# A first stage in another order: squares summed per part, one product to spread a row, both halves of a modulation product in one block

## The chip, the cores and the metric

The kernel runs on one core of a Trainium2 chip. Its engines each take their own instructions in the order in which the program gives them and wait for one another by semaphores: TensorE (PE; its weight loads are shown as PEld), VectorE (DVE), ScalarE (ACT), GpSimd (POOL) and SyncE (SP), which here only issues DMA transfers. The metric is the device time of one execution in microseconds.

## The reference, cut to what matters

One block of a hybrid network over 256 latent tokens, with 256 context tokens ahead of one branch. The change lies in the first lines: the modulation by c, the RMS norm, and the first 1024 columns of the input projection, which alone are needed for both streams.

```python
mod = silu(c) @ w_ada + b_ada                       # (1, 6144): shift, scale, gate
shift, scale, gate = split(mod, 3)                  # mod_c the same from c_ctx
h  = _rmsnorm(x,   norm_g) * (1.0 + scale)   + shift    # x:   256 x 2048
hc = _rmsnorm(ctx, norm_g) * (1.0 + scale_c) + shift_c  # ctx: 256 x 2048
cols = _split_cols(h @ w_in)                        # 13312 columns
xa_c = hc @ w_in[:, :1024]
# RG-LRU over (xa_c, cols[0]), pooling mixer, conformer convolution, each gated by SiLU,
# three projections merged by sigmoid gates, output projection, then
x = x + gate * out
return _rmsnorm(x, final_g)
```

`_rmsnorm(x, g)` is `x * rsqrt(mean(x*x) + 1e-6) * g`. All is float32; a wide product is taken as three products of rounded parts (high x high, high x low, low x high).

## The kernel before, in words

Channels lie on the 128 partitions, in 16 blocks kt of 128 channels; the 512 tokens (256 latent, 256 context) lie along the free axis. xT holds the transposed input as 16 x 512 floats a partition and comes in four transfers, `x_parts`, of 5, 5, 4 and 2 blocks (L376 to L378). cin, 16 KB, holds c and c_ctx; a tanh on ACT (L388) and two operations on DVE make the SiLU of it in sc.

The first stage is one straight list of instructions (`manual_schedule`), so the order of the code is the order on each engine:

1. Squares of each part on ACT (L446), summed over the part's blocks on DVE by a tree of additions, and added to `fold` (L441 to L454).
2. `ada_mm("A", 0)`: half of the product of sc with the modulation weights of block 0, eight matmuls in four column groups. Four small products of `fold` with ones give each token's sum (`tok`, L459); DVE and ACT make the reciprocal root `rt` of it (L461, L462). `ada_mm("B", 0)` is the other half. `keep_warm` issues products that nobody reads.
3. Four times, the diagonal of `rt` and a product with ones (L468, L469) spread one 128-token piece of the row over all partitions; ACT copies it to `rows`.
4. `modulation(kt)` sums the four column groups (L414, L415) and makes shift and gain of a block; `modulate(kt)` multiplies xT by `rows`, applies gain and shift, and splits the result into hH (rounded, ACT) and hL (the rest, DVE).
5. For each kt, seven output tiles of 128 channels: `mm3` issues the three products of a tile, 128x512 each, one behind the other into the same PSUM bank (L239 to L241). Between tiles stand `ada_mm("A", kt + 2)`, `ada_mm("B", kt + 2)` and the modulation of kt + 1.

`Feed` loads weights in a fixed list from SP: each item has a slot, and a load is issued when the slot's holder has been released. `feed.split` makes the rounded and the rest part of a loaded item (ACT, then DVE).

After this stage a list of steps works on the rest of the projections, with the other branches' work in the background of DVE and ACT. The order of these instructions is the same in both kernels.

Of the kernel before, what the change touches and what calls it, by code (L numbers as in the profile page):

```python
# [13 lines left out]
ALU = mybir.AluOpType  # L14

P = 128
D = 2048
KT = 16
L = 256
EPS = 1e-6  # L20
WINDOWS = (2, 4, 8, 16)
NXA = 7
# [12 lines left out]
A_SQ0, A_XT, A_H, A_S, A_RAW = 0, 8192, 16384, 17408, 17920  # L35
# [110 lines left out]
def hybrid_block_kernel(  # L146
# [22 lines left out]
    nc = tc.nc  # L169
# [64 lines left out]
    def split(H, Lo, src):  # L234
        A.copy(H, src)  # L235
        tt(Lo, src, H.bitcast(F32), ALU.subtract)
# [134 lines left out]
    with tc.manual_schedule():  # L371

        cin = sml[:, 0:32]
        nc.sync.dma_start(cin, cc)
        xT = ar[:, A_XT:A_XT + 8192].rearrange("p (k s) -> p k s", k=KT)
        x_parts = ((0, 5), (5, 10), (10, 14), (14, 16))  # L376
        for a, b in x_parts:
            nc.sync.dma_start(xT[:, a:b, :], xt[:, a:b, :])  # L378
        nc.sync.dma_start(vt, vec)
        feed.load()  # L380

# [14 lines left out]
        def mod_ps(kt):  # L396
            return mod_bank[:, 256 * (kt % 2):256 * (kt % 2 + 1)]

        def ada_mm(part, kt):
            i = p1_items[part, kt]  # L400
            ps = mod_ps(kt)
            raw = feed.items[i]["raw"].rearrange("p (k c) -> p k c", c=256)
            for q in range(8):
                k = q if part == "A" else 8 + q
                j = k % 4
                T.matmul(ps[32 * j:32 * j + 32, :], sc[:, k, :], raw[:, q, :], start=k < 4, stop=k >= 12)  # L406
            feed.release(i)
            if part == "B":
                A.copy(S_t[kt % 2], ps)

        def modulation(kt):
            ps = mod_ps(kt)
# [6 lines left out]
            ts(gg, ps[:, 2:4], vt[:, V_BSC + kt:V_BSC + kt + 1], 1.0, op0=ALU.add, op1=ALU.add)  # L419
            ts(gg, gg, vt[:, V_G + kt:V_G + kt + 1], None)  # L420

        def modulate(kt):
            b0 = 80 + 8 * (kt % 2)
            sh, gg = sml[:, b0:b0 + 2], sml[:, b0 + 2:b0 + 4]
            h = h_t[kt % 2]
            tt(h, xT[:, kt, :], rows, ALU.mult)
            for s in range(2):
                hs = h[:, 256 * s:256 * (s + 1)]
                ts(hs, hs, gg[:, s:s + 1], sh[:, s:s + 1])
            split(hH[:, kt, :], hL[:, kt, :], h)  # L430

        warm = bank()

        def keep_warm(n):

            for _ in range(n):
                T.matmul(warm, ones, xT[:, 10, :], start=True, stop=True)
# [3 lines left out]
        tok = bank()  # L441
        for n, (a, b) in enumerate(x_parts):
            k = b - a
            o = A_SQ0 + 2560 * (n % 2)
            sq = ar[:, o:o + 512 * k]
            A.activation(sq, xT[:, a:b, :].rearrange("p k s -> p (k s)"), AF.Square)  # L446
            while k > 1:
                m = k // 2
                tt(sq[:, 0:512 * m], sq[:, 0:512 * m], sq[:, 512 * (k - m):512 * k], ALU.add)
                k -= m  # L450
            if n == 0:
                V.tensor_copy(fold, sq[:, 0:512])
            else:
                tt(fold, fold, sq[:, 0:512], ALU.add)  # L454
        feed.limit = len(feed.items)
        keep_warm(3)
        ada_mm("A", 0)
        for t in range(4):
            T.matmul(tok[:, 2 * t:2 * t + 2], fold[:, P * t:P * (t + 1)], ones[:, 0:2], start=True, stop=True)  # L459
        var, rt, tmp = sml[:, 64:68], sml[:, 68:72], sml[:, 72:76]  # L460
        ts(var, tok[:, 0:8].rearrange("p (t s) -> p t s", s=2)[:, :, 0], 1.0 / D, EPS)  # L461
        rsqrt_newton(rt, var, tmp, rt)  # L462
        ada_mm("B", 0)
        keep_warm(3)
        row_ps = bank()
        for t in range(4):
            w = slice(P * t, P * (t + 1))
            ts(fold[:, w], ident, rt[:, t:t + 1], None)  # L468
            T.matmul(row_ps[:, w], ones, fold[:, w], start=True, stop=True)  # L469
        feed.split(p1_items["X", 0], sub, 1)  # L470
        A.copy(rows, row_ps)
        modulation(0)
        modulate(0)
        feed.split(p1_items["X", 0], sub)
        ada_mm("A", 1)


        xa_ps = [bank() for _ in range(6)] + [small_bank() for _ in range(NXA - 6)]
        for kt in range(KT):
            wh, wl = feed.items[p1_items["X", kt // 2]]["parts"][kt % 2]  # L480
            for t in range(NXA):
                w = slice(P * t, P * (t + 1))
                mm3(xa_ps[t], wh[:, w], wl[:, w], hH[:, kt, :], hL[:, kt, :], kt == 0, kt == KT - 1)
                if t == 1 and kt == 0:
                    ada_mm("B", 1)
                if t == (3 if kt == 0 else 0) and kt + 1 < KT:
                    modulation(kt + 1)
                    modulate(kt + 1)
                    if kt % 2 == 1:
                        feed.split(p1_items["X", (kt + 1) // 2], sub)  # L490
                if t == 0 and kt == KT - 1:
                    feed.split(steps[0][2], sub)
                if t == (4 if kt == 0 else 3) and kt + 2 < KT:
                    ada_mm("A", kt + 2)
            if kt + 2 < KT:
                ada_mm("B", kt + 2)


        xap = [ar[:, A_XAP + 518 * t:A_XAP + 518 * (t + 1)].rearrange("p (s l) -> p s l", s=2) for t in range(8)]
# [712 lines left out]
```

## Time and profile before

| | us |
|---|---|
| median of 3 runs (973.13 to 975.0) | 974.91 |
| the profiled execution's own time | 974.82 |
| its span | 973.0 |
| PE busy in the span | 946.5 (97%) |
| DVE busy | 743.3 (76%) |
| ACT busy | 492.8 (51%) |
| first wide product of the first stage starts at | 28.67 |
| first product of the steps behind it starts at | 149.43 |

The span is what the instructions of the profile cover; some 1.8 us of the execution lie around it. Times in the profile are counted from the start of the span. A line such as L210 or L84 is often that of a helper, so the names of the tiles tell more than the line.

### The profile page before, as it was taken

The page shows a single profiled execution, that of the slowest core. Times are in us where ns is not written, and L with a number is a line of the kernel's source. Part 1 is how long each engine was busy: PE and PEld are TensorE (multiplying, and loading weights), DVE is VectorE, ACT ScalarE, POOL GpSimd, SP SyncE. Part 2 cuts the span into 40 slices and gives each one's busy share as a digit, 9 for nine tenths or more (in the row PEclk, how much of TensorE's full clock was granted, in tenths as well). Part 3 has the DMA queues.
Part 4 walks back from the last instruction along what each step waited for, and adds up shares of the span by engine and source line. Part 5 has one row for each costly group of instructions (what it writes and reads, how often), then busy time and mean ns, then how long its engine had stood idle before and what let it go on. Part 6 is the DMA issues. An engine that isn't in the chain of part 4 may idle for free.

```text
span 973.0 us, 18156 instructions
## 1 busy us (share of the span) xinstructions
PE 946.5 (97%) x7561; PEld 876.6 (90%) x7561; DVE 743.3 (76%) x1143; ACT 492.8 (51%) x641; POOL 40.7 (4%) x74
## 2 busy tenths in 40 slices
PE   4999999999999999999999999999999999999996
PEld 2666668999999999999999999999999999998885
DVE  5445456876976785899999999996666888898764
ACT  4222226566656767674445544444675444444442
POOL 0000010000100000000000000000002011101000
PEclk9999999999999999999999999999999999999998
DMA  9998854554545555455555555555569788878642
GB/s 369 372 416 319 347 191 167 213 173 162 192 168 185 182 187 177 169 186 176 215 180 210 177 213 178 208 180 190 173 204 357 262 320 318 307 262 308 201 173 87
DMA packets 34722, 220.70 MB, mean 227 GB/s; under 512 B 4128, under 2 KB 4272, under 8 KB 11856
## 3 DMA queue, kind: packets, MB, share of 16 engines
q1 hardware_dynamic: 28080, 195.28, 55.1%
q0 software_dynamic: 6560, 24.26, 7.2%
q8 instruction: 59, 0.97, 0.4%
q14 instruction: 23, 0.19, 0.1%
HBM read 217.43 MB, written 2.10 MB: 226 GB/s over the span
## 4 chain that ended last, share of the span: by engine, by line
PE 95%; DVE 2%; DMA 1%; ACT 1%; issue 0%; SPq 0%; ACTq 0%; DVEq 0%
PE acc L265 24%; PE acc L266 24%; PE acc L269 24%; PE sm L406 3%; PE acc L239 3%; PE acc L1100 3%; PE acc L1098 3%; PE acc L1101 3%; PE acc L240 2%; PE acc L241 2%; PE sm L240 1%; DVE ar L210 1%; PE sm L239 1%; PE sm L241 1%; DMA ar<-in_xt_dram 1%; PE acc L960 0%
## 5 line engine op out<-in xcount | busy, mean ns | idle before, releaser
L265 PE MATMUL acc<-hH,wh 128*128 128x256 f32 (+1 forms) x2000 | 466.8, 278 | 0.0
L266 PE MATMUL acc<-hL,wh 128*128 128x256 f32 (+1 forms) x2000 | 464.6, 277 | 0.0
L84 ACT CAST wh<-raws 128x1024 fp32r<-128x1024 f32 (+1 forms) x288 | 298.2, 1050 | 261.5 <-PE acc L266 222.6
L210 DVE TENSOR_TENSOR wl<-raws,wh 128x1024 fp32r<-128x1024 f32 (+1 forms) x288 | 339.7, 1218 | 108.6 <-ACT wh L84 55.5
L265 PEld LDWEIGHTS acc<-hH,wh 128*128 128x128 f32 x2000 | 375.6, 188 | 1.7
L266 PEld LDWEIGHTS acc<-hL,wh 128*128 128x128 f32 x2000 | 375.7, 188 | 0.7
L269 PE MATMUL acc<-hH,wl 128*128 128x256 f32 (+1 forms) x2000 | 253.4, 277 | 0.0
L269 PEld LDWEIGHTS acc<-hH,wl 128*128 128x128 f32 x2000 | 239.5, 188 | 0.7
L221 DVE SCALAR_TENSOR_TENSOR ar<-ar,vt 128x256 f32<-128x256 f32 (+1 forms) x264 | 115.3, 503 | 0.0
L210 DVE TENSOR_TENSOR ar<-ar 128x512 f32<-128x512 f32 (+6 forms) x136 | 87.4, 665 | 7.9 <-ACT ar L446 6.2
L221 DVE SCALAR_TENSOR_TENSOR ar<-ar,sc 128x512 f32<-128x512 f32 x64 | 48.1, 751 | 16.4 <-DMA ar<-in_w_gate_dram 15.0
L235 ACT CAST hH<-ar 128x256 fp32r<-128x256 f32 (+1 forms) x68 | 31.5, 491 | 53.3 <-DVE ar L217 47.0
L210 DVE TENSOR_TENSOR hL<-ar,hH 128x256 fp32r<-128x256 f32 (+1 forms) x76 | 39.5, 547 | 22.7 <-ACT hH L235 22.7
L1100 PE MATMUL acc<-wh,hH 128*128 128x512 f32 (+1 forms) x144 | 51.8, 369 | 0.0
L1101 PE MATMUL acc<-wh,hL 128*128 128x512 f32 (+1 forms) x144 | 51.3, 366 | 0.0
L239 PE MATMUL acc<-hH,wh 128*128 128x512 f32 x96 | 42.5, 442 | 1.2 <-ACT hH L235 1.2
L215 DVE TENSOR_SCALAR sml<-sm,vt 128x2 f32<-128x2 f32 x16 | 3.5, 220 | 48.5 <-PE sm L415 48.5
L240 PE MATMUL acc<-hL,wh 128*128 128x512 f32 x96 | 38.2, 398 | 0.3 <-DVE hL L210 0.2
L241 PE MATMUL acc<-hH,wl 128*128 128x512 f32 x96 | 37.9, 395 | 0.0
L239 PEld LDWEIGHTS acc<-hH,wh 128*128 128x128 f32 x96 | 18.0, 188 | 16.0 <-issue 11.9
L1098 PE MATMUL acc<-wl,hH 128*128 128x512 f32 (+1 forms) x144 | 32.1, 366 | 0.0
L1101 PEld LDWEIGHTS acc<-wh,hL 128*128 128x128 f32 x144 | 27.0, 188 | 4.8 <-issue 0.2
(142 smaller groups left out, 662.4 us busy)
## 6 DMA issues: line engine op xcount, KB each, us to landing
raws<-in_w_br_dram SPq DMA_DIRECT2D x49, 1024.0 KB, 4.9
raws<-in_w_gl_dram SPq DMA_DIRECT2D x48, 1024.0 KB, 4.9
raws<-in_w_bout_dram SPq DMA_DIRECT2D x24, 1024.0 KB, 4.9
raws<-in_w_ada_dram SPq DMA_DIRECT2D x16, 1024.0 KB, 8.9
ar<-in_w_ada_dram SPq DMA_DIRECT2D x16, 1024.0 KB, 8.8
ar<-in_w_gate_dram POOLq DMA_DIRECT2D x32, 512.0 KB, 5.7
raws<-in_w_out_dram SPq DMA_DIRECT2D x16, 1024.0 KB, 5.0
ar<-in_w_xa_dram SPq DMA_DIRECT2D x5, 896.0 KB, 11.7
```

The source lines that it names most:

```text
L84: self.nc.scalar.copy(h[:, 0:w], src)
L210: V.tensor_tensor(out=o, in0=a, in1=b, op=op)
L221: V.scalar_tensor_tensor(o, a, s, b, op0=op0, op1=op1)
L239: T.matmul(ps, sh, mh, start=start, stop=False)
L240: T.matmul(ps, sh, ml, start=False, stop=False)
L241: T.matmul(ps, sl, mh, start=False, stop=stop)
L265: T.matmul(ps, wh[k], mh[k], start=k == 0, stop=False)
L266: T.matmul(ps, wh[k], ml[k], start=False, stop=False)
L269: T.matmul(ps, wl[k], mh[k], start=False, stop=k == len(wh) - 1)
L1098: T.matmul(ps, H, wl[:, w], start=False, stop=kt == KT - 1)
L1100: T.matmul(ps, H, wh[:, w], start=kt == 0, stop=False)
L1101: T.matmul(ps, Lo, wh[:, w], start=False, stop=False)
```

## The change

The transfer of cin is issued behind the four parts of xT and not ahead of them. The sums of squares are no longer added up in `fold`: each part's sum goes through its own four token products, and a reduction on DVE adds the four results. Each part has its own room for the squares. One multiplication on DVE makes the four diagonals, and one 128x512 product spreads the row. Both halves of `ada_mm` stand in one block; the multiplication of xT by the row is issued one block ahead (`scaled`), for block 0 straight from PSUM. The first weights are split behind block 0's modulation. The wide products of a block run over the seven tiles for each of the three pairs of operands.

```diff
-        nc.sync.dma_start(cin, cc)
         x_parts = ((0, 5), (5, 10), (10, 14), (14, 16))
         for a, b in x_parts:
             nc.sync.dma_start(xT[:, a:b, :], xt[:, a:b, :])
+        nc.sync.dma_start(cin, cc)
...
+        def ada_mm(kt):
             ps = mod_ps(kt)
+            for part in "AB":
...
+            A.copy(S_t[kt % 2], ps)
...
+        def scaled(kt, by):
+            tt(h_t[kt % 2], xT[:, kt, :], by, ALU.mult)
...
             split(hH[:, kt, :], hL[:, kt, :], h)
+            if kt + 1 < KT:
+                scaled(kt + 1, rows)
...
-            o = A_SQ0 + 2560 * (n % 2)
+            o = (A_SQ0, A_SQ0 + 2560, A_SQ0 + 5120, A_H)[n]
...
+            for t in range(4):
+                c = 8 * n + 2 * t
+                T.matmul(tok[:, c:c + 2], sq[:, P * t:P * (t + 1)], ones[:, 0:2], start=True, stop=True)
             if n == 0:
-                V.tensor_copy(fold, sq[:, 0:512])
-            else:
-                tt(fold, fold, sq[:, 0:512], ALU.add)
+                keep_warm(2)
...
-        keep_warm(3)
-        ada_mm("A", 0)
...
+        V.tensor_reduce(var, tok[:, 0:32].rearrange("p (n t s) -> p t n s", n=4, t=4)[:, :, :, 0],
+                        axis=mybir.AxisListType.X, op=ALU.add)
+        ts(var, var, 1.0 / D, EPS)
         rsqrt_newton(rt, var, tmp, rt)
-        ada_mm("B", 0)
-        keep_warm(3)
+        tt(fold.rearrange("p (t c) -> p t c", t=4), ident[:, None, :].to_broadcast([P, 4, P]),
+           rt[:, :, None].to_broadcast([P, 4, P]), ALU.mult)
+        keep_warm(2)
         row_ps = bank()
-        for t in range(4):
-            w = slice(P * t, P * (t + 1))
-            ts(fold[:, w], ident, rt[:, t:t + 1], None)
-            T.matmul(row_ps[:, w], ones, fold[:, w], start=True, stop=True)
-        feed.split(p1_items["X", 0], sub, 1)
+        T.matmul(row_ps, ones, fold, start=True, stop=True)
+        ada_mm(0)
+        scaled(0, row_ps)
+        modulation(0)
         A.copy(rows, row_ps)
-        modulation(0)
         modulate(0)
         feed.split(p1_items["X", 0], sub)
-        ada_mm("A", 1)
...
+            at_ada, at_mod = ((5, 20), 10) if kt == 0 else ((13,), 2)
+            for i in range(3 * NXA):
+                a, t = divmod(i, NXA)
+                T.matmul(xa_ps[t], (wh, wh, wl)[a][:, P * t:P * (t + 1)], (hH, hL, hH)[a][:, kt, :],
+                         start=kt == 0 and a == 0, stop=kt == KT - 1 and a == 2)
```

On SP, at the start of the program; cc is cin's tensor, xt the input, vec the small vectors.

```order
-L374 DMA sml<-in_cc_dram 128x32
-L378 DMA ar<-in_xt_dram 128x2560 x2
-L378 DMA ar<-in_xt_dram 128x2048
-L378 DMA ar<-in_xt_dram 128x1024
+L1210 UNCONDITIONAL_BRANCH
+L377 DMA ar<-in_xt_dram 128x2560 x2
+L377 DMA ar<-in_xt_dram 128x2048
+L377 DMA ar<-in_xt_dram 128x1024
+L378 DMA sml<-in_cc_dram 128x32
 L379 DMA vt<-in_vec_dram 128x424
```

The small transfer now stands fifth, behind the 4 MB of xt; its line alone has moved.

On PE, the start of the program before; L437 is `keep_warm`, L406 `ada_mm`, L459 the token products, L469 the row, acc_197 and acc_198 the first output tiles.

```order
L437 MATMUL acc_105<-ar,ones 128x512 x3
L406 MATMUL sm_104<-raws,sc 32x256 x8
L459 MATMUL acc_106<-ones,ar 128x2 x4
L406 MATMUL sm_104<-raws,sc 32x256 x8
L437 MATMUL acc_105<-ar,ones 128x512 x3
L469 MATMUL acc_160<-ar,ones 128x128 x4
L414 MATMUL sm_104<-sel_75,ar 128x2
L415 MATMUL sm_104<-sel_75,ar 128x2
L406 MATMUL sm_104<-raws,sc 32x256 x8
L239 MATMUL acc_197<-hH,wh_0_169 128x512
L240 MATMUL acc_197<-hL,wh_0_169 128x512
```

The same place now; L457 are the token products, L441 `keep_warm`, L470 the row, L407 `ada_mm`, L485 the wide products.

```order
L457 MATMUL acc_106<-ones,ar 128x2 x4
L441 MATMUL acc_105<-ar,ones 128x512 x2
L457 MATMUL acc_106<-ones,ar 128x2 x12
L441 MATMUL acc_105<-ar,ones 128x512 x2
L470 MATMUL acc_149<-ar,ones 128x512
L407 MATMUL sm_104<-raws,sc 32x256 x16
L414 MATMUL sm_104<-sel_75,ar 128x2
L415 MATMUL sm_104<-sel_75,ar 128x2
L485 MATMUL acc_190<-hH,wh_0_182 128x512
L485 MATMUL acc_191<-hH,wh_0_182 128x512
L485 MATMUL acc_192<-hH,wh_0_182 128x512
```

Both halves of block 0's modulation product, 16 matmuls, now stand behind the row's product instead of ahead of it, and block 1's has left the start.

On PE, a piece from the middle of the stage before, from the last tile of one block into the next.

```order
L241 MATMUL acc_202<-hH,wl_1_504 128x512
L239 MATMUL sm_203<-hH,wh_1_503 128x512
L240 MATMUL sm_203<-hL,wh_1_503 128x512
L241 MATMUL sm_203<-hH,wl_1_504 128x512
L406 MATMUL sm_104<-ar,sc 32x256 x8
L239 MATMUL acc_197<-hH,wh_0_608 128x512
L240 MATMUL acc_197<-hL,wh_0_608 128x512
L241 MATMUL acc_197<-hH,wl_0_609 128x512
L414 MATMUL sm_104<-sel_75,ar 128x2
L415 MATMUL sm_104<-sel_75,ar 128x2
L239 MATMUL acc_198<-hH,wh_0_608 128x512
L240 MATMUL acc_198<-hL,wh_0_608 128x512
```

The like piece now.

```order
L485 MATMUL sm_196<-hL,wh_0_610 128x512
L407 MATMUL sm_104<-ar,sc 32x256 x16
L485 MATMUL acc_190<-hH,wl_0_611 128x512
L485 MATMUL acc_191<-hH,wl_0_611 128x512
L485 MATMUL acc_192<-hH,wl_0_611 128x512
L485 MATMUL acc_193<-hH,wl_0_611 128x512
L485 MATMUL acc_194<-hH,wl_0_611 128x512
L485 MATMUL acc_195<-hH,wl_0_611 128x512
L485 MATMUL sm_196<-hH,wl_0_611 128x512
L485 MATMUL acc_190<-hH,wh_1_614 128x512
L485 MATMUL acc_191<-hH,wh_1_614 128x512
L485 MATMUL acc_192<-hH,wh_1_614 128x512
```

A block's modulation product is one run of 16 matmuls instead of two runs of 8, with wide products on either side, and neighbouring wide products go to different banks with the same moving operand.

## Rows read from the trace of the kernel before

**Rows 1.** The page's part 4: the chain that ended last, shares by engine.
```profile
PE 95%; DVE 2%; DMA 1%; ACT 1%; issue 0%; SPq 0%; ACTq 0%; DVEq 0%
```

**Rows 2.** Timeline, first 30 us, DMA issues of SP; start, duration, engine, line, form.
```profile
0.74 0.39 SPq L374 DMA_DIRECT2D sml<-in_cc_dram  x1
...
1.18 1.92 SPq L378 DMA_DIRECT2D ar<-in_xt_dram  x4
```

**Rows 3.** DMA view, window 0 to 60 us: issues, KB each, us to landing.
```profile
raws<-in_w_xa_dram SPq DMA_DIRECT2D x1, 896.0 KB, 4.3
ar<-in_xt_dram SPq DMA_DIRECT2D x1, 512.0 KB, 11.3
vt<-in_vec_dram SPq DMA_DIRECT2D x1, 212.0 KB, 11.3
```

**Rows 4.** Timeline, 2 to 20 us, squares and their trees; idle time and releaser in brackets.
```profile
2.36 0.23 ACT L388 ACTIVATE sml<-sml 128x32 f32<-128x32 f32 x1 [0.34 <-DMA sml<-in_cc_dram]
...
6.90 2.34 ACT L446 ACTIVATE ar<-ar 128x2560 f32<-128x2560 f32 x1 [4.31 <-DMA ar<-in_xt_dram]
9.27 2.68 DVE L210 TENSOR_TENSOR ar<-ar 128x1024 f32<-128x1024 f32 x3 [6.17 <-ACT ar L446]
...
12.52 7.32 DVE L210 TENSOR_TENSOR ar<-ar 128x1024 f32<-128x1024 f32 x9
...
12.76 4.76 PE L437 MATMUL acc<-ar,ones 128*128 128x512 f32 x6 [12.76 <-DMA ar<-in_xt_dram]
...
16.01 1.06 ACT L446 ACTIVATE ar<-ar 128x1024 f32<-128x1024 f32 x1 [1.37 <-DVE ar L210]
...
17.08 1.28 ACT L277 ACT_TABLE_LOAD   x1
...
19.89 1.05 PE L459 MATMUL acc<-ones,ar 128*128 128x2 f32 x8 [1.38 <-DVE ar L210]
```

**Rows 5.** Timeline, 21 to 30 us, from the token products to the first wide product.
```profile
21.88 2.84 PE L437 MATMUL acc<-ar,ones 128*128 128x512 f32 x6
22.02 0.37 ACT L409 COPY ar<-sm 128x256 f32<-128x256 f32 x1 [0.63 <-PE sm L406]
...
22.43 0.87 DVE L215 TENSOR_SCALAR ar<-ident,sml 128x128 f32<-128x128 f32 x4
...
25.34 0.30 PEld L414 LDWEIGHTS sm<-sel,ar 128*128 128x128 f32 x2
...
25.99 0.22 DVE L215 TENSOR_SCALAR sml<-sm,vt 128x2 f32<-128x2 f32 x1 [1.64 <-PE sm L415]
...
26.51 0.68 DVE L210 TENSOR_TENSOR ar<-ar 128x512 f32<-128x512 f32 x1
...
28.00 0.62 ACT L235 CAST hH<-ar 128x512 fp32r<-128x512 f32 x1 [1.77 <-DVE ar L217]
28.53 0.94 ACT L84 CAST wh<-ar 128x896 fp32r<-128x896 f32 x1
...
28.67 0.50 PE L239 MATMUL acc<-hH,wh 128*128 128x512 f32 x1 [1.21 <-ACT hH L235]
...
29.40 0.50 PE L240 MATMUL acc<-hL,wh 128*128 128x512 f32 x1 [0.23 <-DVE hL L210]
```

**Rows 6.** Timeline of PE, 90 to 93 us: one border between two kinds of product.
```profile
90.25 0.40 PE L241 MATMUL acc<-hH,wl 128*128 128x512 f32 x1
90.49 0.39 PE L239 MATMUL sm<-hH,wh 128*128 128x512 f32 x1
...
90.95 0.39 PE L241 MATMUL sm<-hH,wl 128*128 128x512 f32 x1
91.27 1.07 PE L406 MATMUL sm<-ar,sc 128*32 128x256 f32 x16
92.27 0.50 PE L239 MATMUL acc<-hH,wh 128*128 128x512 f32 x1
92.61 0.40 PE L240 MATMUL acc<-hL,wh 128*128 128x512 f32 x1
```

More of the change, by code (lines that the diff above doesn't have):

```diff
@@ L397, in mod_ps @@
             return mod_bank[:, 256 * (kt % 2):256 * (kt % 2 + 1)]
-        def ada_mm(part, kt):
-            i = p1_items[part, kt]
+        def ada_mm(kt):
             ps = mod_ps(kt)
[L402 to L409, printed above, removed]
+            for part in "AB":
+                i = p1_items[part, kt]
+                raw = feed.items[i]["raw"].rearrange("p (k c) -> p k c", c=256)
+                for q in range(8):
+                    k = q if part == "A" else 8 + q
+                    j = k % 4
+                    T.matmul(ps[32 * j:32 * j + 32, :], sc[:, k, :], raw[:, q, :], start=k < 4, stop=k >= 12)
+                feed.release(i)
+            A.copy(S_t[kt % 2], ps)
         def modulation(kt):
@@ L425, in modulate @@
             h = h_t[kt % 2]
-            tt(h, xT[:, kt, :], rows, ALU.mult)
             for s in range(2):
@@ L450, in hybrid_block_kernel @@
                 k -= m
+            for t in range(4):
+                c = 8 * n + 2 * t
+                T.matmul(tok[:, c:c + 2], sq[:, P * t:P * (t + 1)], ones[:, 0:2], start=True, stop=True)
             if n == 0:
-                V.tensor_copy(fold, sq[:, 0:512])
-            else:
-                tt(fold, fold, sq[:, 0:512], ALU.add)
+                keep_warm(2)
         feed.limit = len(feed.items)
-        keep_warm(3)
-        ada_mm("A", 0)
-        for t in range(4):
-            T.matmul(tok[:, 2 * t:2 * t + 2], fold[:, P * t:P * (t + 1)], ones[:, 0:2], start=True, stop=True)
         var, rt, tmp = sml[:, 64:68], sml[:, 68:72], sml[:, 72:76]
-        ts(var, tok[:, 0:8].rearrange("p (t s) -> p t s", s=2)[:, :, 0], 1.0 / D, EPS)
+        V.tensor_reduce(var, tok[:, 0:32].rearrange("p (n t s) -> p t n s", n=4, t=4)[:, :, :, 0],
+                        axis=mybir.AxisListType.X, op=ALU.add)
+        ts(var, var, 1.0 / D, EPS)
         rsqrt_newton(rt, var, tmp, rt)
-        ada_mm("B", 0)
-        keep_warm(3)
+        tt(fold.rearrange("p (t c) -> p t c", t=4), ident[:, None, :].to_broadcast([P, 4, P]),
+           rt[:, :, None].to_broadcast([P, 4, P]), ALU.mult)
+        keep_warm(2)
         row_ps = bank()
-        for t in range(4):
-            w = slice(P * t, P * (t + 1))
-            ts(fold[:, w], ident, rt[:, t:t + 1], None)
-            T.matmul(row_ps[:, w], ones, fold[:, w], start=True, stop=True)
-        feed.split(p1_items["X", 0], sub, 1)
+        T.matmul(row_ps, ones, fold, start=True, stop=True)
+        ada_mm(0)
+        scaled(0, row_ps)
+        modulation(0)
         A.copy(rows, row_ps)
-        modulation(0)
         modulate(0)
         feed.split(p1_items["X", 0], sub)
-        ada_mm("A", 1)
         xa_ps = [bank() for _ in range(6)] + [small_bank() for _ in range(NXA - 6)]
@@ L480, in hybrid_block_kernel @@
             wh, wl = feed.items[p1_items["X", kt // 2]]["parts"][kt % 2]
[L481 to L496, printed above, removed]
+            at_ada, at_mod = ((5, 20), 10) if kt == 0 else ((13,), 2)
[3 more added lines that the diff above has]
+                         start=kt == 0 and a == 0, stop=kt == KT - 1 and a == 2)
+                if i in at_ada:
+                    k = 1 if i == 5 else kt + 2
+                    if k < KT:
+                        ada_mm(k)
+                if i == at_mod:
+                    if kt + 1 < KT:
+                        modulation(kt + 1)
+                        modulate(kt + 1)
+                        if kt % 2 == 1:
+                            feed.split(p1_items["X", (kt + 1) // 2], sub)
+                    else:
+                        feed.split(steps[0][2], sub)
         xap = [ar[:, A_XAP + 518 * t:A_XAP + 518 * (t + 1)].rearrange("p (s l) -> p s l", s=2) for t in range(8)]
```

## The prediction

> **What bounds the kernel now.** I read the chain of waits first: PE holds 95% of it [rows 1], so what counts is PE's time, and the time for which PE cannot start. Then the timeline of the first 30 us, for the second: the first wide product of the first stage starts at 28.67 [rows 5], and until then a chain through several engines sets the end. The reader should follow it: the input lands, the first square starts at 6.90, the DVE trees run without a gap from 12.52 to 19.84 (12.52 + 7.32), the token products follow at 19.89 [rows 4], then small DVE work, the row, and block 0's modulation [rows 5]. Last I read a piece of PE's timeline inside the stage, where PE has no gap: there a change counts only by the product starts that it takes out or adds [rows 6].
>
> **The transfer of cin.** SP issues cin at 0.74 and the four parts of the input from 1.18 to 3.10 [rows 2]. Moving cin behind them makes the input 0.44 earlier (1.18 - 0.74). But the tanh of cin is the first activation on ACT. It started at 2.36, released by this transfer [rows 4], and the program keeps it ahead of the four squares. ACT does not pass a waiting instruction: the table load at 17.08 waits for nothing that is computed, and yet stood behind the last square, which waited 1.37 for DVE [rows 4]. So the squares now wait for cin, and cin's landing decides.
>
> The queue serves transfers in the order of issue as far as rows show: the last input part landed 11.3 after its issue, at about 2.6 + 11.3 = 13.9; the small vectors (212 KB), issued right behind at 3.1, landed also 11.3 later, at 14.4, instead of soon after their issue [rows 2, 3]. cin now stands between these two. It lands between 13.9 - 0.44 = 13.5 and 14.0; I take 13.65, nearer to the lower end as it has 16 KB. The tanh takes 0.23, so the first square starts at 13.9 instead of 6.90.
>
> The Trainium skill, page DMA: Bandwidth & Descriptors, section Queues, rings and completion order, has a rule for each side: on one DMA engine the descriptors of a queue are taken in ring order, but completion is not FIFO per issuing engine, since a later transfer on fewer engines may be complete first. By the first cin lands behind the input, and the vectors' row agrees; by the second it could land early, which is the first rival below, at 971.8.
>
> **Squares and trees.** The first square ends at 13.9 + 2.34 = 16.24. The trees then bind, because all squares follow each other on ACT faster than DVE sums them (2.34 against 2.68 for a part of five). First tree 2.68, to 18.95. The other nine operations took 7.32 [rows 4], three of them additions into fold, which are gone: with 0.69 each (a 128x512 operation took 0.68 [rows 5]) 5.25 are left. The last sum is there at 24.2, not at 19.84: the fold additions save 2.07 and the gap on DVE ahead of the second tree closes, but the start is 7.0 later.
>
> **From the last sum (T = 24.2) to the first wide product.** Before, 28.67 - 19.84 = 8.8. Now, step by step. Only the last part's four token products lie behind T: 1.1 with the start (1.05 [rows 4]). The reduction over four parts is new; no row shows it on PSUM, and I take 0.2, since the six small operations from 20.94 (end of the token products) to 22.43 took 1.49, a quarter each; at 0 or at 0.7 (a whole 128x512 operation) the sum shifts by -0.2 or +0.5. Those 1.49 stay: T + 2.8. One 128x512 operation for the four diagonals, 0.7 where four took 0.87 [rows 5]: T + 3.5. keep_warm (two products) fits under this DVE work. The row's product is one f32 128x512, as in keep_warm, three of which took 2.84 [rows 5], so 0.95: T + 4.45. Then both halves of block 0's modulation product, 1.0 each (91.27 to 92.27 [rows 6]), which before lay beside DVE work, now on the path: T + 6.45. The copy of it on ACT 0.37 and its start: T + 6.9. From the load of L414 to DVE 0.65 (25.34 to 25.99): T + 7.55; the copy of the row, 0.6 on ACT, lies beside this. From there to the rounding of h took 2.0 (25.99 to 28.00), less the product with the row, 0.7, which is now done under the modulation product: T + 8.85. ACT then rounds h and behind it the first weights, which before were split much earlier: that operation starts 0.53 after the other and takes 0.94 [rows 5], T + 10.35, PE at T + 10.4 = 34.6. Against 28.67 the stage starts 5.9 later.
>
> **Inside the stage.** A product start follows the last by 0.23 to 0.24, whether the operand changes in one bank (90.49 to 90.95, two) or bank and weights change too (90.25 to 90.49) [rows 6]. So I give the new order of operands nothing; a difference of 0.02 either way would be 336 x 0.02 = 6.7, but no row has one. A run of eight modulation matmuls takes 1.0, yet from the wide start ahead of it to the second one behind it 92.61 - 90.95 = 1.66 pass, where two products alone would take 0.47: 1.19, so 0.19 a run is border. Before, 29 runs lie behind the first wide product; now 15 runs of double length: 14 x 0.19 = 2.7 saved. Block 1's first half, before ahead of the first wide product while PE waited, now costs 1.0. The wait for hL at the second product (29.40 - 28.67 = 0.73, where a border takes 0.34) falls away, as six products with hH come first: 0.4 saved. Sum -2.1. Modulation of the next block keeps the same two products and has over 5 us of cover on DVE and ACT, more than the 3 us that it takes.
>
> At the end all seven tiles finish within the last seven products, 1.6 us, so ACT's copies out of PSUM start about 2.5 later against the stage's end. The next step's 48 products of 0.23, 11 us, hide this: nothing. If that cover failed, the cost would be those 2.5.
>
> **Sum.** +5.9 - 2.1 = +3.8 on the profiled execution's 974.82 (span 973.0 and 1.8 around it; 0.1 below the median of 974.91): 978.6.
>
> **Rivals.**
> Not slower: cin lands early, as before 1.6 us after its issue, because a small transfer is not held by those ahead. Decided by whether the tanh starts before 6.5. Then the second tree starts at 12.52 - 0.44 = 12.08, T is 17.33, the first wide product at 27.7, 0.95 earlier than before, and with the -2.1 the time is 971.8. For it: cin's own quick landing [rows 4], but with nothing ahead of it; against it: the vectors' 11.3 [rows 3]. 0.08.
>
> Slower still, by the clock: PE's first work is now the first part's token products at about 19, not keep_warm at 12.76. In the rows keep_warm's first six halves took 4.76, the later six 2.84 [rows 4, 5]; 0.79 and 0.47 each; the first were slow at the start of PE's work (the low level, 1.2 GHz), the later, after it had been busy, fast (2.4 GHz). If PE is still at the low level at T, keep_warm's four halves take 3.2 instead of 1.9 and end 0.8 after the diagonals, the row costs 0.6 more and the modulation product up to 2.0 more: +3.4, 982.0. Against it: some 5 us of almost steady PE work lie between 19 and T, as from 12.76 to 17.5 before. 0.10. The Trainium skill, page TensorE: Matmul & The Clock Gate, Part 1, says the same of the two levels, that the slow one is the default and activity releases it; by it too the start of the activity matters, and no row shows this one.
>
> Slower by the weights: block 1's second half and all behind it are issued only when block 0's first half is released, at T + 5.45 = 29.7, instead of under the small work. A transfer of this kind alone in the queue took 4.3 [rows 3], so it lands at 34, ahead of its use at 37 (six products and the first half behind 34.6). But the loads for blocks 2 and 3 then queue up behind block 1's release, all within a few us; if one comes late, PE waits for a part of a transfer, up to 2 of its 4.3: 980.6. 0.10.
>
> The blocks do not do what they say: a run of 16 has the same borders as two of 8. Then 2.7 are not saved: 981.3. Against it: the border is seen only where kinds of product meet [rows 6]. 0.05.
>
> **How the numbers follow.** The forecast has 0.67, and a range of its own of 977 to 980.3 from cin's landing, the reduction and the weights. What a measurement here can tell from no change is 0.2%, 1.95 us. Faster needs the first rival, or cin early and part of the rest: 0.09. Same, 973 to 976.9, needs a term half as large, such as a square start near 11: 0.08. Slower: 0.83. The range for 8 in 10 is 975 to 982, which leaves out the early cin and little above.
>
> **What would show it.** Right: the tanh on ACT starts at 13.5 to 14, released by cin's transfer, the first square behind it; DVE's trees without a gap to about 24; first wide product near 34.6; one run of 32 modulation records a block; the first product of the later steps about 3.8 later than 149.43. Wrong: a tanh before 7, a product start that is not 0.23, or a PE gap ahead of a modulation product.

## The result, and the profile after

The changed kernel took 984.49 us (median of five, 980.87 to 987.25) against 974.91 before (973.13 to 975.61): a ratio of 1.0097 [1.0069, 1.0124], 9.6 us slower. The forecast was 978.6, in a range of 975 to 982. Run again later, the same kernel took 982.27 against 976.92 for the kernel before, a ratio of 1.0057 [1.0037, 1.0077]. Its direction was as forecast, its size was not.

The profiled execution is the fastest of the five: 980.87, span 979.1. It is 2.3 above the forecast, and all that follows on places and durations is read from it. First the timeline of its first 42 us (start, duration, engine, line, form; idle time and releaser in brackets). L450 are the squares, L457 the token products, L441 `keep_warm`, L470 the row, L407 the modulation product, L485 the wide products.

```profile
2.64 0.44 SPq L378 DMA_DIRECT2D sml<-in_cc_dram  x1
...
13.31 0.23 ACT L388 ACTIVATE sml<-sml 128x32 f32<-128x32 f32 x1 [11.30 <-DMA sml<-in_cc_dram]
13.45 7.29 ACT L450 ACTIVATE ar<-ar 128x2560 f32<-128x2560 f32 x4
...
15.80 7.73 DVE L210 TENSOR_TENSOR ar<-ar 128x1024 f32<-128x1024 f32 x9 [1.74 <-ACT ar L450]
...
18.63 1.84 PE L457 MATMUL acc<-ones,ar 128*128 128x2 f32 x8 [18.63 <-DVE ar L210]
...
20.33 3.76 PE L441 MATMUL acc<-ar,ones 128*128 128x512 f32 x4
...
23.88 3.03 PE L457 MATMUL acc<-ones,ar 128*128 128x2 f32 x24
...
26.77 2.67 PE L441 MATMUL acc<-ar,ones 128*128 128x512 f32 x4
26.94 0.17 DVE L462 TENSOR_REDUCE sml<-acc 128x4 f32<-128x16 f32 x1 [3.41 <-PE acc L457]
...
29.35 2.08 PE L470 MATMUL acc<-ar,ones 128*128 128x512 f32 x2
...
31.35 1.93 PE L407 MATMUL sm<-raws,sc 128*32 128x256 f32 x32
...
35.96 0.62 ACT L235 CAST hH<-ar 128x512 fp32r<-128x512 f32 x1 [1.74 <-DVE ar L217]
36.48 1.78 ACT L84 CAST wh<-ar 128x896 fp32r<-128x896 f32 x2
...
37.47 2.38 PE L485 MATMUL acc<-hH,wh 128*128 128x512 f32 x6 [3.08 <-ACT wh L84]
...
39.78 2.56 PE L407 MATMUL sm<-raws,sc 128*32 128x256 f32 x28
```

Against [rows 2, 4, 5] the reader sees three things. SP issues cin at 2.64 instead of 0.74, so the tanh starts at 13.31 instead of 2.36, released by cin's transfer, and the four squares stand behind it. The last tree ends at 15.80 + 7.73 = 23.53 instead of 19.84. And from there to the first wide product 13.9 us pass (37.47 - 23.53) where 8.8 did before; the row's two records alone take 2.08, and the first six wide products and block 1's modulation product, which stand behind, are slow too. At which clock they ran is in the windows of the same stretch (columns: window, its length, busy time of PE, PEld, DVE, ACT and POOL, granted clock, DMA share, GB/s):

```profile
26.00:27.00 1.00, 1.00 (x10) 1.00 (x10) 0.06 (x1) 0.00 (x0) 0.00 (x0) 1.00 0.00 0
...
28.00:29.00 1.00, 1.00 (x2) 0.00 (x0) 0.89 (x4) 0.00 (x0) 0.00 (x0) 0.50 0.00 0
...
36.00:37.00 1.00, 0.00 (x0) 0.00 (x0) 0.39 (x1) 1.00 (x2) 0.00 (x0) 1.00 1.07 451
...
40.00:41.00 1.00, 1.00 (x12) 0.40 (x8) 0.00 (x0) 0.00 (x0) 0.00 (x0) 0.50 0.00 0
```

The granted clock is at 0.50, which is 1.2 of 2.4 GHz, from 28 to 31, across the row, and again from 38 to 41, across the wide products and the run at 39.78. Ahead of the first fall PE had been busy without a gap from 20 on, with `keep_warm`, twelve token products and `keep_warm` again; ahead of the second it had waited 3.08 for the weights and run its first wide products. In the kernel before, the granted clock reads 1.00 in every one of these windows. Up to its first fall the record reads 1.00 in the kernels here, also where PE's first products are slow (20.33, 3.76 for four records, as in [rows 4]); it does not show the low level of the start.

The DMA view of 0 to 40 us answers [rows 3] (issues, KB, us to landing):

```profile
vt<-in_vec_dram SPq DMA_DIRECT2D x1, 212.0 KB, 10.6
sml<-in_cc_dram SPq DMA_DIRECT2D x1, 16.0 KB, 10.6
```

cin lands 10.6 after its issue, as the vectors behind it do.

Then the stage itself, in the chain (start, duration, piece), two blocks of the kernel after:

```profile
60.48 1.86 PE sm L407 x32
62.34 1.59 PE acc L485 x6
...
67.88 1.86 PE sm L407 x32
```

and the same view of the kernel before, where L406 is the modulation product and L239 a wide product:

```profile
60.38 1.00 PE sm L406 x16
61.38 0.43 PE acc L239
...
64.83 1.00 PE sm L406 x16
...
68.12 1.00 PE sm L406 x16
```

A block takes 7.40 (67.88 - 60.48) and took 7.74 (68.12 - 60.38). The joined run takes 1.86 where two took 1.00 each, and one border is left where there were two. The first product of the later steps starts at 155.73 (149.43 before), so the stage, from its first wide product at 37.47 (28.67), takes 118.26 instead of 120.76. From there to the end of the span it is 823.4 (823.6 before).

### The profile page after: what moved, and what is told of

The parts are those of the page before. It is cut to its first block, busy times and chain, and to the rows that moved or that the text cites. A ratio compares the mean times of both kernels' runs of the same rounds, so it can differ in the third digit from the quotient of the medians.

```text
span 979.1 us, 18179 instructions
## 1 busy us (share of the span) xinstructions
PE 945.7 (97%) x7575; PEld 881.8 (90%) x7575; DVE 738.5 (75%) x1137; ACT 491.7 (50%) x641; POOL 40.6 (4%) x74
## 4 chain that ended last, share of the span: by engine, by line
PE 95%; DMA 2%; DVE 1%; ACT 1%; issue 0%; SPq 0%; ACTq 0%; DVEq 0%
PE acc L265 24%; PE acc L266 23%; PE acc L269 23%; PE acc L485 7%; PE sm L407 3%; PE acc L1100 3%; PE acc L1102 3%; PE acc L1103 3%; DMA sml<-in_cc_dram 1%; DMA ar<-in_w_ada_dram 1%; PE sm L485 1%; PE sm L240 1%; PE sm L239 1%; PE sm L241 1%; PE acc L441 1%; DVE ar L210 1%
## 5 line engine op out<-in xcount | busy, mean ns | idle before, releaser
L265 PEld LDWEIGHTS acc<-hH,wh 128*128 128x128 f32 x2000 | 375.6, 188 | 1.6
L210 DVE TENSOR_TENSOR ar<-ar 128x512 f32<-128x512 f32 (+5 forms) x132 | 83.3, 655 | 3.3 <-ACT ar L450 1.7
L485 PE MATMUL acc<-hH,wh 128*128 128x512 f32 x96 | 29.3, 418 | 3.1 <-ACT wh L84 3.1
L1102 PEld LDWEIGHTS acc<-wh,hH 128*128 128x128 f32 x144 | 27.0, 188 | 4.8 <-issue 0.2
L221 DVE SCALAR_TENSOR_TENSOR ar<-ar,acc 128x256 f32<-128x256 f32 (+1 forms) x56 | 29.5, 527 | 0.7 <-ACT ar L901 0.4
L1100 PEld LDWEIGHTS acc<-wl,hH 128*128 128x128 f32 x144 | 25.0, 188 | 4.6
## 6 DMA issues: line engine op xcount, KB each, us to landing
raws<-in_w_ada_dram SPq DMA_DIRECT2D x16, 1024.0 KB, 10.6
```

The lines of the kernel that those rows point to most:

```text
L221: V.scalar_tensor_tensor(o, a, s, b, op0=op0, op1=op1)
L265: T.matmul(ps, wh[k], mh[k], start=k == 0, stop=False)
L485: T.matmul(xa_ps[t], (wh, wh, wl)[a][:, P * t:P * (t + 1)], (hH, hL, hH)[a][:, kt, :], start=kt == 0 and a == 0, stop=kt == KT - 1 and a == 2)
L1100: T.matmul(ps, H, wl[:, w], start=False, stop=kt == KT - 1)
L1102: T.matmul(ps, H, wh[:, w], start=kt == 0, stop=False)
```

## The experiments

All kernels compute the whole result. Each has one trace (the changed kernel two, with e10), from which its places and durations are read. Times are medians; a ratio stands against the kernel before on the same chip. The kernel before took 974.99 beside the first four runs (972.89 to 980.41, 29 runs), 976.23 beside the next four (973.77 to 979.32, 29) and 976.92 beside the last four (972.57 to 981.89, 25).

**Where cin's transfer stands.** Four kernels: the changed one with cin first again, the kernel before with cin late, and two in which the input still goes first on SP's queue and only the wait of the squares is taken away.

```diff
# e1_cin_first: the changed kernel
+        nc.sync.dma_start(cin, cc)
         for a, b in x_parts:
             nc.sync.dma_start(xT[:, a:b, :], xt[:, a:b, :])
-        nc.sync.dma_start(cin, cc)
# e2_before_cin_late: the kernel before, the same two lines the other way round
# e3_tanh_behind: the changed kernel; behind the loop of the squares, no longer ahead of it
         A.activation(cth, cin, AF.Tanh, scale=0.5)
         stt(cth, cth, 1.0, cin, ALU.add, ALU.mult)
         ts(sc[:, :, 0:2], cth.rearrange("p (k s) -> p k s", s=2), 0.5, None)
# e4_cin_other_queue: the changed kernel
+        nc.gpsimd.dma_start(cin, cc)
         for a, b in x_parts:
             nc.sync.dma_start(xT[:, a:b, :], xt[:, a:b, :])
-        nc.sync.dma_start(cin, cc)
```

> The changed kernel with one line put back: cin's transfer ahead of the input again. Theory A (the loss comes from cin landing behind the input and holding ACT's squares): tanh near 2.4, first square near 6.9, first wide product near 28, and 968 to 972. Rival B (the new order at the start, with the token products queued behind keep_warm and both halves of the modulation product on the path, costs as much by itself): first wide product at 31 or later, 975 to 979. Rival C (the new order of the wide products makes the stage slower or unsteady): a stage of more than 120.8 from its first wide product, 977 or more, and as wide a spread of times as the changed kernel's 980.9 to 987.3.

> The kernel before with one line of the change: cin's transfer behind the input. Theory A: tanh near 13.3, squares one behind the other, the sum of squares near 26, first wide product near 35, time 980 to 985. Rivals B and C, by which the line alone does little: 974 to 977.

> The changed kernel with the transfer of cin left behind the input, but the tanh and the two DVE operations behind it put behind the squares and their trees, where they are needed only by the modulation product of block 0. If it is ACT's order that turns the late landing into a loss (theory A): first square near 6.45, first wide product near 27.5, 967 to 972, as with cin first or up to 0.4 better. If the late transfer costs in another way (the queue, the weights behind it): 975 or more.

> The changed kernel with cin's transfer issued from GpSimd at the start, so that SP issues the input at once. If cin was late because SP's queue serves in the order of issue: it lands by 4, first square near 6.5, 967 to 972. If the 16 engines are simply full and any later small transfer waits: it lands late as well, and the time is that of the changed kernel, 980 to 987.

Measured: e1 976.25 (973.28 to 979.06, 12 runs), 1.0004 [0.9986, 1.0023]; e2 985.76 (983.58 to 987.06, 5), 1.0105 [1.0084, 1.0126]; e3 975.60 (973.00 to 979.32, 12), 1.0012 [0.9996, 1.0029]; e4 975.37 (972.08 to 978.86, 10), 0.9993 [0.9976, 1.0011]. Timeline of e2, the tanh, the token products and the first wide product:

```profile
13.57 0.23 ACT L388 ACTIVATE sml<-sml 128x32 f32<-128x32 f32 x1 [11.55 <-DMA sml<-in_cc_dram]
...
26.48 1.87 PE L459 MATMUL acc<-ones,ar 128*128 128x2 f32 x8 [8.71 <-DVE ar L210]
...
38.24 0.49 PE L239 MATMUL acc<-hH,wh 128*128 128x512 f32 x1 [1.20 <-ACT hH L235]
```

and of e4, tanh, first square, first wide product:

```profile
6.69 0.23 ACT L388 ACTIVATE sml<-sml 128x32 f32<-128x32 f32 x1 [4.67 <-DMA sml<-in_cc_dram]
6.83 2.32 ACT L450 ACTIVATE ar<-ar 128x2560 f32<-128x2560 f32 x1
...
30.46 2.51 PE L485 MATMUL acc<-hH,wh 128*128 128x512 f32 x6 [3.08 <-ACT wh L84]
```

The one moved line makes the kernel before 10.8 us slower, as much as the whole change at its first measurement (9.6) and more than at its second (5.4); its first wide product starts 9.6 later (38.24, before 28.67). Of these, 6.6 lie ahead of the token products (26.48, before 19.89). The other 3.0 lie behind them: PE had waited 8.71 there, and the granted clock reads 0.50 from 23 to 32, so that the four token products take 1.87 instead of 1.05. Taking the line back, or the tanh, or the queue that cin shares with the input, brings the changed kernel back to no difference from before. So the loss needs both: cin behind 4 MB on one queue, and the squares behind the tanh on ACT. From the other queue cin's tanh starts at 6.69, and the first square right behind it at 6.83.

What these four also show, as rival B of e1 had it: without the late cin the new kernel isn't faster. e1, whose trees end at 17.51 (12.37 + 5.14), 2.3 before the old ones, starts its first wide product at 32.86, 4.2 later than the old kernel (2.2 later, at 30.88, in e7 below, which has the same start):

```profile
13.82 3.76 PE L441 MATMUL acc<-ar,ones 128*128 128x512 f32 x4
17.37 5.12 PE L457 MATMUL acc<-ones,ar 128*128 128x2 f32 x24
22.35 3.61 PE L441 MATMUL acc<-ar,ones 128*128 128x512 f32 x4
25.80 1.02 PE L470 MATMUL acc<-ar,ones 128*128 128x512 f32 x2
...
32.86 2.93 PE L485 MATMUL acc<-hH,wh 128*128 128x512 f32 x6 [3.08 <-ACT wh L84]
```

Twelve token products take 5.12 here, `keep_warm`'s four records still 3.61 at 22.35 (four records at the later pace of [rows 5]: 1.9), and the row at 25.80 is the first to run at the fast pace, though PE was busy without a gap from 12.12 on. Then PE waits 3.08 and the next six products are slow again.

**What PE does before the stage.** If it is the slow PE that eats the gain, early big products should mend it (e5); if it is the order of the row and the modulation product, moving that product under the small DVE work should (e6, which also rounds the first weights ahead of block 0's modulation). e7 takes the products in their old order by tiles, e8 puts the start of before ahead of the new stage, without block 1's first half. All four have cin first.

```diff
# e5_cin_first_warm_first: e1 and
+        keep_warm(3)
         for n, (a, b) in enumerate(x_parts):
...
-            if n == 0:
-                keep_warm(2)
# e6_start_regrouped: e5 and
         rsqrt_newton(rt, var, tmp, rt)
+        ada_mm(0)
...
-        keep_warm(2)
         row_ps = bank()
         T.matmul(row_ps, ones, fold, start=True, stop=True)
-        ada_mm(0)
...
+        A.copy(x0h[:, 0:x0["w"]], x0["raw"][:, 0:x0["w"]])
         scaled(0, row_ps)
...
# e7_cin_first_tile_order: e1 and
-                a, t = divmod(i, NXA)
+                t, a = divmod(i, 3)
# e8_stage_only: e1 and the start of before (sums in fold, four row products)
+        keep_warm(3)
+        ada_mm(0, "A")
         for t in range(4):
             T.matmul(tok[:, 2 * t:2 * t + 2], fold[:, P * t:P * (t + 1)], ones[:, 0:2], start=True, stop=True)
...
+        ada_mm(0, "B")
+        keep_warm(3)
...
```

> cin first, and three keep_warm products ahead of all other work of PE instead of two behind the first part's token products. With cin first alone the sum of squares was there at 17.5, as the first rival of the prediction had it, but the first wide product came at 32.9, not 27.7: the last twelve token products took 5.12 us and the keep_warm behind them 3.61, which is the pace of the low clock. Theory D (PE is at the low clock because sparse small products do not raise it): the sixteen token products now take 2.0 to 2.3 in all, the reduction starts at 19.5 to 20, first wide product 28.5 to 30, 971 to 974. Rival E (the token products queue behind keep_warm whatever the clock): reduction at 22 or later, first wide product at 32 or later, 975 to 978.

> A version put together from the findings: cin first, three keep_warm first, squares per part without the additions into fold, both halves of the modulation product of block 0 between the token products and the row (beside the small DVE work, and PE busy), one product for the row, the rounding of the first weights ahead of block 0's modulation, the changed kernel's stage. By theories A and D: first wide product 24.5 to 26.5, stage 117 to 118.5, time 966 to 969. By E the start stays near 29 or later: 971 or more. If the weights are the next bound, the stage shows waits of PE for w_ada and is longer than 119.

> cin first, with the wide products in the old order (the three products of a tile one behind the other) and the modulation product still one run of 16. In the changed kernel a block took 7.40 (60.48 to 67.88 in the chain), before 7.74. If the gain is the run of 16 alone (1.86 where two runs of 8 took 1.0 each, and one border less): 7.40 here too. If the order of operands has a part in it: 7.45 to 7.74. At the start of the stage the wait for hL at the second product comes back.

> The start of the kernel before (cin first, fold, ada halves ahead of the row, four row products) with the changed kernel's stage. If the changed stage is a gain of its own: first wide product near 28.7 as before, stage near 116.5 against 120.8, time 969 to 972. If what it gains is given back later or lost in waits for weights: 973 to 976.

Measured: e5 977.29 (976.12 to 979.32, 12 runs), 1.0011 [1.0000, 1.0023]; e6 974.46 (972.95 to 978.00, 12), 0.9992 [0.9977, 1.0006]; e7 981.32 in its one run; e8 972.26, 0.9959 [0.9946, 0.9972] (the median is of 12 runs; the ratio leaves out one of them, 1062.48; the others lie at 970.99 to 975.28). PE's rows of e5, then of e6:

```profile
12.89 5.43 PE L441 MATMUL acc<-ar,ones 128*128 128x512 f32 x6 [12.89 <-DMA ar<-in_xt_dram]
18.14 3.72 PE L458 MATMUL acc<-ones,ar 128*128 128x2 f32 x32
21.73 3.58 PE L441 MATMUL acc<-ar,ones 128*128 128x512 f32 x4
...
32.20 2.93 PE L484 MATMUL acc<-hH,wh 128*128 128x512 f32 x6 [3.08 <-ACT wh L84]
```

```profile
21.64 3.25 PE L407 MATMUL sm<-raws,sc 128*32 128x256 f32 x32
...
28.73 2.92 PE L489 MATMUL acc<-hH,x0h 128*128 128x512 f32 x6 [2.44 <-ACT hH L235]
31.58 3.40 PE L407 MATMUL sm<-raws,sc 128*32 128x256 f32 x32
```

e5 refutes the half of the theory by which early big products bring the start forward. The token products do run at the fast pace behind six early products (32 records in 3.72, 0.116 each, against 0.21 in e1), but all sixteen then queue behind the early `keep_warm`, and the next `keep_warm` is slow again (3.58 for four). The first wide product comes at 32.20 only. e6 brings it to 28.73, where the old kernel has it, but the modulation products then take 3.25 and 3.40 instead of 1.86, and the later steps start at 149.34, as before (149.43).

e7 answers the term that I gave nothing, the order of the products. Its chain:

```profile
63.85 1.86 PE sm L407 x32
...
71.25 1.86 PE sm L407 x32
```

71.25 - 63.85 = 7.40, to the hundredth the block of the changed kernel. The order by operands is worth nothing here; the 0.34 come from the joined run and the border that it saves. Its first stage has waits of its own (0.76 for the second weights ahead of its third product, and 3.64 for block 1's run at the low clock), but its later steps start at 151.69, only 0.7 later than in e1 (151.00). The other 2.9 by which its span is longer than that of e1 (979.5, 975.9) lie behind; there PE waits 2.88 ahead of a product of the gate at 776.43 (e1: 1.10), and the clock reads 0.50 from 776 to 782. From one run I claim no more.

e8 is the first version clearly faster than before, with its first wide product at 30.26.

**The new stage behind the whole old start, the change once more, and two attempts to keep PE at pace.** e9 adds block 1's first half to e8's start, which makes the start of before complete. e10 is the changed kernel. e11 keeps cin late and fills PE's time with `keep_warm`. e12 is e9 with cin on the other queue and block 0 multiplied by the row straight from PSUM, ahead of its modulation.

```diff
# e9_old_start_new_stage: e8 and, ahead of the stage
         feed.split(p1_items["X", 0], sub)
+        ada_mm(1, "A")
...
-                        ada_mm(k)
+                        ada_mm(k, "B" if k == 1 else "AB")
# e11_cin_late_kept_busy: the changed kernel and
+        keep_warm(5)
         for n, (a, b) in enumerate(x_parts):
...
-            if n == 0:
-                keep_warm(2)
+            if n < 2:
+                keep_warm(1)
...
         modulate(0)
+        keep_warm(3)
# e12_other_queue_old_start: e9 and
-        nc.sync.dma_start(cin, cc)
+        nc.gpsimd.dma_start(cin, cc)
...
+        scaled(0, row_ps)
         modulation(0)
-        scaled(0, rows)
```

> The stage-alone kernel with block 1's first half of the modulation product put back ahead of the first wide product, where PE idles: the start is now that of the kernel before to the instruction, the stage the changed one. In the stage-alone run the first wide product came at 30.3, the first six took 2.3 and block 1's run 2.9, at a granted clock of 0.83. If it is the idle time ahead of the stage that drops the clock (theory D): 1.0 in 20 to 40, first wide product near 28.7, stage near 116, time 968.5 to 970.5. If the clock drops all the same: 971 to 973.

> The changed kernel once more, beside the others on one chip: 981 to 987. Its first profile was its fastest execution (980.9). If slower ones differ by the clock at the start, the granted clock in 20 to 50 is lower here, or low for longer, and the first wide product is at 38 or later or the first blocks take longer; if they differ by waits for weights, PE shows more than 0.4 of waits for w_ada.

> The changed kernel with cin left behind the input and PE kept busy: five keep_warm products ahead of all, one behind each of the first two parts' token products, three more while PE waits ahead of the first wide product. If the prediction's sum was right but for the low clock and the token products that queue behind keep_warm: the last token product ends near 25.1 and not 26.9, the row takes 1.0 and not 2.1, first wide product 34 to 35 (the predicted 34.6), time 975.5 to 978.5. If the late squares cost more than that by themselves: 980 or more.

> As the kernel with the old start and the changed stage, with cin's transfer issued from GpSimd so that the input starts 0.44 earlier, and block 0 multiplied by the row straight from PSUM ahead of its modulation: 967.5 to 970, 0.4 to 0.7 less than that one if the start still sets the end, the same if the weights do.

Measured: e9 969.74 (969.32 to 972.86, 6 runs), 0.9928 [0.9902, 0.9954]; e10 982.27 (980.85 to 983.03, 8), 1.0057 [1.0037, 1.0077]; e11 979.64 (975.41 to 982.91, 12), 1.0028 [1.0010, 1.0046]; e12 970.50 (968.32 to 976.94, 12), 0.9940 [0.9921, 0.9960]. PE's rows of e9:

```profile
19.72 1.05 PE L464 MATMUL acc<-ones,ar 128*128 128x2 f32 x8 [0.46 <-DVE ar L210]
...
21.70 2.84 PE L442 MATMUL acc<-ar,ones 128*128 128x512 f32 x6
...
26.22 1.07 PE L407 MATMUL sm<-raws,sc 128*32 128x256 f32 x16 [0.44 <-DVE sml L217]
28.49 2.75 PE L490 MATMUL acc<-hH,wh 128*128 128x512 f32 x6 [1.21 <-ACT hH L235]
```

These stand where they stood before: token products at 19.72 (19.89), `keep_warm` at 21.70 (21.88), the first wide product at 28.49 (28.67). The later steps start at 145.25, so the new stage takes 116.8 and gains 4.0, even with its first six products slow (2.75; the clock fell to 0.50 between 28 and 32 here, where the kernel before, with the same work on PE up to this point, kept 1.00). This version beats both kernels. Of the 7.2 between the medians the trace places 4.2 (145.25 against 149.43). Its profiled run is its slowest, 972.86; the other five lie at 969.32 to 970.61. This run lost 2.3 behind the first stage (825.9, before 823.6), in part at the gate's product, ahead of which PE waits 2.11 (0.88 before) and whose two records then take 1.87 (1.10 before); what the faster five did there no trace shows. e12, for which I had expected 0.4 to 0.7 less, is not told apart from e9. In its profiled run (975.00) the first wide product comes at 30.23, 1.7 later than in e9, with the clock at 0.50 from 21 to 23.

e10 repeats the pattern: token products at 18.83, row 2.08 at 29.68, first wide product at 37.83. Its later steps start at 156.15, 0.4 later than in the first profile; the rest of its longer time (983.03) lies behind the first stage, where it takes 1.7 more for the same work. The place is a stretch of like steps, of which these are two runs of eight products each, first of e10, then of the first profile:

```profile
858.55 1.11 PE L269 MATMUL acc<-hH,wl 128*128 128x256 f32 x8
...
861.38 1.10 PE L269 MATMUL acc<-hH,wl 128*128 128x256 f32 x8
```

```profile
848.47 1.07 PE L269 MATMUL acc<-hH,wl 128*128 128x256 f32 x8
...
851.19 1.07 PE L269 MATMUL acc<-hH,wl 128*128 128x256 f32 x8
```

From one such run to the next, a step takes 2.83 in e10 (861.38 - 858.55) and 2.72 in the first profile (851.19 - 848.47), both at a granted clock of 1.00 and with PE busy throughout; some 16 steps at 0.11 more would make the 1.7 (an estimate). So a part of the spread between executions is a slower pace of PE in steps that the change does not touch, and its cause stays open.

e11, PE's rows and one window:

```profile
23.19 2.32 PE L458 MATMUL acc<-ones,ar 128*128 128x2 f32 x16
...
28.92 1.92 PE L471 MATMUL acc<-ar,ones 128*128 128x512 f32 x2
...
37.16 1.67 PE L487 MATMUL acc<-hH,wh 128*128 128x512 f32 x6 [0.41 <-ACT wh L84]
```

```profile
26.00:27.00 1.00, 1.00 (x2) 0.34 (x1) 0.67 (x4) 0.17 (x1) 0.00 (x0) 0.50 0.00 0
```

The last token products end at 25.5 (23.19 + 2.32) instead of 26.9, as the queue explanation wants, and the six wide products behind the added `keep_warm` are fast (1.67 instead of 2.38). But they start at 37.16, where I had expected 34 to 35. Behind the token products the clock is at 0.50 from about 25 to 31 although PE was busy without a gap, and the row takes 1.92, where I had expected 1.0. Filling PE's time gave back 2.6 by the medians on the same chip (979.64 against e10's 982.27), not the whole loss.

## Why the prediction was right in its direction and short in its size

**Right: cin.** The tanh was forecast at 13.65 and came at 13.31; the first square at 13.9 came at 13.45, the end of the trees at 24.2 came at 23.53. e1 to e4 show both halves of the argument, the queue and ACT's order. The first rival (cin lands early) fell: 16 KB behind 4 MB landed 10.6 after its issue, behind nothing 1.6 (the kernel before) and 1.8 (e1). The rule of the Trainium skill (DMA: Bandwidth & Descriptors, section Queues, rings and completion order) that descriptors are taken in ring order is the one with which this row agrees; that a later transfer of the same queue may be complete first is shown by no run here.

**Wrong: "From the last sum (T = 24.2) to the first wide product".** I had 10.4; it took 13.9. The failed step in it is "Only the last part's four token products lie behind T: 1.1". They took 3.4 (23.53 to 26.91). What the forecast overlooked stands in the order on PE that it had itself: `keep_warm` follows the first part's products, and the twelve of the other three parts follow `keep_warm`. That block started at 20.33 and, at PE's slow pace of the start, took 3.76 to 23.9, past T; then all twelve ran, 3.03. Order and pace both belong to it: at the 1.9 that the forecast gave these two products, the block would have ended near 22.2, ahead of T (an estimate from 20.33 and [rows 5]), and e11, where PE is at the fast pace by then, ends the token products 1.4 earlier. That is +2.3 of the 2.9 by which the first wide product is late against the forecast 34.6.

**Wrong, with a chance of 0.10: the clock at T.** The rival "Slower still, by the clock" gave 982.0, which lies nearest to the result. The row took 2.0 instead of 0.95 (+1.05), worse than its +0.6; `keep_warm` took 2.67 for its four records and not 3.2, and ended beside the diagonals (29.44 and 29.29), so it cost nothing; the modulation product of block 0 was at pace (1.93). So its sum was not what happened, and that its number lies near is luck. Its condition, a low level that lasts from the start to T, held just up to T: PE's products run at the fast pace from 23.88, just behind T (24 records in 3.03), as my argument against it had it, 5 us of almost steady PE work ahead of T. But that argument took a busy PE for a held clock: PE was busy, half of the time at the slow pace and then with 128x2 products, and the clock fell at about 28 all the same, here as in e11 at about 25. The rule of the Trainium skill (TensorE: Matmul & The Clock Gate, Part 1) that activity releases the throttle agrees with the early `keep_warm` of e5, behind which the token records run at 0.116. In e1, where PE was busy from 12.12 on, they still took 0.21 each.

The two terms, less the 0.67 by which T came earlier and with 0.2 of small differences, make the +2.9.

**The stage: right in sign, mis-sized.** Forecast -2.1, measured -2.5, in spite of slow products at its start (2.38 for the first six, where six at pace take 1.59, and 2.7 from 39.78 to the end of block 1's run, where 1.86 would do). The border is 0.19 as read from [rows 6]; what the forecast lacked is that the joined run is itself shorter, 1.86 instead of 2 x 1.00. That makes 0.33 or 0.34 a block, over 14 blocks 4.7 instead of 2.7. In e9, where block 1's first half stays ahead of the stage, the stage comes to -4.0. The order of the products is worth nothing (e7), as forecast. The rival "weights late" cost 0.42 at one place (53.87), not 2; the rival without saved borders fell.

**The sum.** Against the profiled execution: first wide product +2.9, stage -0.4, behind it -0.2, together the 2.3 between 978.6 and 980.87. Against the median of 984.49 another 3.6 are missing, a spread between executions of which e10's slower steps show one part (1.7) and no trace here the cause. By ratios on their chips: cin's place costs 0.5 to 0.9% (e10 or the first measurement against e1), the new start 0.8% against the old one (e1 against e9), and the new stage gives 0.7% back (e9). The three steps lead from one kernel to the other, so that they add up says nothing by itself; the e2 run, which has the first alone on the other kernel, does say something: 1.05%.

What I took too lightly: I costed the new start piece by piece at one pace of PE. Even with cin early it is 4.2 later (e1) or 2.2 later (e7) at the first wide product than the old one, which had `keep_warm` and a run of 128x256 ahead of its few token products, and whose modulation product lay under DVE's work.

## What to carry to other kernels

A transfer's place in its queue counts by the first instruction that waits for it and by all that stands behind that instruction on its engine: 16 KB moved behind the input cost 10.8 us in the kernel before, of which 3.0 by the first wide product lie behind PE's wait, at the low clock. Where products are moved to "as early as their data is there", read what stands ahead of them in the engine's own order, and at which pace, before giving them to the cover. And an edit with several parts wants its parts measured alone: the useful one here, the new stage with its joined runs, measured -0.7% behind the old start (e9) and stood under two that together cost more.

## What the runs showed of the hardware that I had not expected

- A run of 32 records of 128x256 into four column groups took 1.86, two runs of 16 records 1.00 each.
- Twelve token products (24 records of 128x2) took 5.12 in e1 and 2.94 in e7, which give PE the same instructions up to there, and 3.03 in the changed kernel. The kernel before, e8, e9 and e12 give PE the same instructions up to the row; the granted clock fell at about 21 in e8 and e12, at about 29 in e9, and not at all up to 50 in the kernel before. So when the clock rises and falls is not settled by the program alone.
- The granted clock was at 0.50 from about 25 to 31 in e11 with PE recorded as busy throughout, behind 128x2 products. A busy PE in the profile does not say that the clock holds.
- At a granted clock of 1.00 and with PE busy throughout, like steps of 128x256 products took 2.72 in one execution of the changed kernel and 2.83 in another.
- An input of 16 KB issued from GpSimd beside 4 MB on SP's queue landed 5.4 after its issue, on SP's queue behind it 10.6, ahead of it 1.8 (e1).
